# A sum of squares over partitions as two one-pass products of its exact halves

## The chip, the cores and the metric

The kernel runs on one core of one Trainium2 chip. The metric is the device time of one execution in microseconds (us), as the median of several runs. The engines are named TensorE (PE, its weight loads PEld), VectorE (DVE), ScalarE (ACT), GpSimd (POOL) and SyncE (SP).

## The reference

Two consecutive layers of a decoder, on one sequence of 512 tokens of width 1024 in fp32. Layer 0 has four differential-attention heads (A), four forgetting-attention heads (B) and a gate; layer 1 has eight dilated-window heads (C) and a gate. Each layer ends in an output projection, a residual add and a per-layer embedding. The part that matters here is the end of a differential head: two softmax maps are subtracted, applied to the values, and each token's 128 outputs are normalised by the root of their mean square.

```
w = probs(q1b, k1) - lam * probs(q2b, k2)
oa = einsum('bhqk,bkhd->bqhd', w, v)
oa = rms_norm(oa, subln_g) * (1.0 - lam_init)   # mean of squares over 128 values
```

## The kernel before, in words

All large products are made from exact halves. An fp32 operand is split (`split`, L140 to L147) into `hi`, a copy by ScalarE to the type float32r, and `lo`, the remainder, subtracted by VectorE; `mm3` (L173) then adds three float32r products, hi hi, hi lo and lo hi. Each of these is one pass of TensorE over 512 columns. Plain fp32 products remain for transposes, for probabilities times values (L503) and for the normalisation of the differential heads (L521).

The work is a list of jobs (`add_chunk`, L902 to L951). A job is a projection of 512 columns, cut into units, mostly four: one unit is 24 products into one PSUM buffer of the tag U (three buffers, `psU`), and an evacuation, for the query and key units in `qk_post`: L379 copies the PSUM tile to `raw`, L381 squares it. While a job runs, the weights of the next are loaded and split (L143, L144 for layer 0), and heads of attention advance by stages: scores (`scores`, L438, PSUM tag S, two buffers), exponentials (L448), the division by their sums (L480 to L487), transposes (L493, L495), and the product with the values (L503) into PSUM `po`.

`run_jobs` and `slot` fix the order in which the program is written: a slot runs what was deferred to it (`defer`), some attention stages by a planner of costs (`attend`), a share of the weight preparation, then the unit. A scheduler of the framework then orders the instructions of each engine by this order and by its own estimate of when each is ready; each engine executes its queue in order. Work tiles of 128x512 fp32 come from one pool, `t2` (L69), with nine buffers (`T2BUFS`).

When the fourth query block of a differential head is done, `finish_a` (L513) runs. L515 copies `po` to `oc`, L517 squares it to `sq`, both on ScalarE in t2 tiles. One slot later `rest` multiplies `sq` by `onesd`, a 128x128 tile of 1/128 (L118, filled by POOL at L119): the fp32 product L521, in a buffer of the tag S, leaves each token's mean square in all partitions. L523 (VectorE) adds the epsilon, L525 and L526 (ScalarE) take the logarithm and the exponential, giving `y`. One slot later `last` refines `y` by one Newton step (`newton`, L125 to L128) and L531 writes the normalised head. This happens four times, once per A head, between 107 and 189 us of the span, while the projections of the B heads' values, queries and keys run. The heads' results are used by the gate units (L712) much later.

Of the kernel before, what the change touches and what calls it, by code (L numbers as in the profile page):

```python
# [13 lines left out]
F32R = mybir.dt.float32r  # L14
I32 = mybir.dt.int32
AF = mybir.ActivationFunctionType
# [3 lines left out]
P = 128  # L20
# [27 lines left out]
def trunk_kernel(  # L48
# [7 lines left out]
    V, A, G, T = nc.vector, nc.scalar, nc.gpsimd, nc.tensor  # L56
# [8 lines left out]
    def nm(s):  # L65
        cnt[0] += 1
        return f"{s}{cnt[0]}"

    def t2(shape=(P, 512), dt=F32):  # L69
        return sb.tile(list(shape), dt, tag="t2", bufs=T2BUFS, name=nm("t2_"))  # L70
# [10 lines left out]
    def psS():  # L81
        return psum.tile([P, 512], F32, tag="S", bufs=SB, name=nm("ps_"))

    def psX():
        return psum.tile([P, 4, P], F32, tag="X", bufs=XB, name=nm("px_"))

    def psO():
        return psum.tile([P, 512], F32, tag="O", bufs=OB, name=nm("po_"))

    def const(shape, name, dt=F32):  # L90
        return cpool.tile(list(shape), dt, tag=name, name=name)
# [25 lines left out]
    rrow = const([P, 512], "rrow")  # L117
    onesd = const([P, P], "onesd")  # L118
    G.memset(onesd, 1.0 / P)  # L119
    gcols = const([P, 2, KS], "gcols")  # L120
    A.dma_start(out=gcols, in_=norm_g.rearrange("l (k q) -> q l k", q=P))


    def newton(y, ms, tmp):
        V.tensor_tensor(tmp, y, y, op=OP.mult)  # L125
        V.tensor_tensor(tmp, tmp, ms, op=OP.mult)
        V.tensor_scalar(tmp, tmp, -0.5, 1.5, op0=OP.mult, op1=OP.add)
        V.tensor_tensor(y, y, tmp, op=OP.mult)  # L128
# [11 lines left out]
    def split(hi, lo, src, gain=None):  # L140

        if gain is not None:
            A.activation(hi, src, AF.Copy, scale=gain)  # L143
            V.scalar_tensor_tensor(lo, src, gain, hi.bitcast(F32), op0=OP.mult, op1=OP.subtract)  # L144
            return
        A.activation(hi, src, AF.Copy)  # L146
        V.tensor_tensor(lo, src, hi.bitcast(F32), op=OP.subtract)  # L147
# [51 lines left out]
    def defer(n, f):  # L199
        later.setdefault(clock[0] + n, []).append(f)  # L200
# [237 lines left out]
    def scores(qk, qk0, hh, p0, pn, i, bias, pt):  # L438
        n = P * (i + 1)
        ps = psS()  # L440
        if i == 0:
            T.matmul(ps[:, :n], qk0[p0:p0 + pn, 0, hh], qk0[p0:p0 + pn, 1, hh], start=True, stop=True)
        else:
            scores_split(ps, qk, hh, p0, pn, i)
        st_ = sm(3)
        V.tensor_tensor_reduce(out=pt, in0=ps[:, :n], in1=bias, scale=1.0, scalar=BIG,  # L446
                               op0=OP.add, op1=OP.min, accum_out=st_[:, 0:1])
        A.activation(pt, pt, AF.Exp, bias=st_[:, 0:1], scale=-1.0, accum_out=st_[:, 1:2])  # L448
        return st_

    def head_steps(kind, hh, qk, qk0, v, vcol, fin, first, extra=None):
        box = {}

        def ptile():
            return sb.tile([P, 512], F32, tag="P", bufs=PBUFS, name=nm("P"))

        def step(i):
            n = P * (i + 1)
            off = 384 - P * i
            if kind == "b":  # L460
                ck, cq, h = extra
                if i == 0:
                    box["ck"] = t2()
                    nc.sync.dma_start(out=box["ck"], in_=ck[h:h + 1, :].broadcast_to((P, 512)))
                bt = t2()
                V.scalar_tensor_tensor(bt[:, :n], box["ck"][:, :n], cq[:, i, h:h + 1],
                                       consts["causal"][:, off:512], op0=OP.subtract, op1=OP.add)
                bias = bt[:, :n]
            else:
                bias = consts["causal" if kind == "a" else "biasc"][:, off:512]  # L470
            p1 = ptile()[:, :n]
            if kind == "a":
                p2 = ptile()[:, :n]
                s1 = scores(qk, qk0, hh, 0, 64, i, bias, p1)
                s2 = scores(qk, qk0, hh, 64, 64, i, bias, p2)
            else:
                s1 = scores(qk, qk0, hh, 0, P, i, bias, p1)

            def end():
                V.reciprocal(s1[:, 2:3], s1[:, 1:2])  # L480
                if kind == "a":
                    V.reciprocal(s2[:, 2:3], s2[:, 1:2])
                    V.tensor_tensor(s2[:, 2:3], s2[:, 2:3], consts["lam"], op=OP.mult)
                    G.tensor_scalar(p2, p2, s2[:, 2:3], 0.0, op0=OP.mult, op1=OP.add)
                    V.scalar_tensor_tensor(p1, p1, s1[:, 2:3], p2, op0=OP.mult, op1=OP.subtract)
                else:
                    G.tensor_scalar(p1, p1, s1[:, 2:3], 0.0, op0=OP.mult, op1=OP.add)  # L487
                defer(LAG2, stage2)

            def stage2():  # L490
                px = psX()
                for j in range(i + 1):
                    T.transpose(px[:, j, :], p1[:, j * P:(j + 1) * P], ident)  # L493
                pt = sb.tile([P, 4, P], F32, tag="pt", bufs=PTBUFS, name=nm("pt"))
                A.activation(pt[:, :i + 1, :], px[:, :i + 1, :], AF.Copy)  # L495
                defer(LAG3, lambda: stage3(pt))

            def stage3(pt):
                if i == 0:
                    box["o"] = psO()  # L500
                po = box["o"]
                for j in range(i + 1):
                    T.matmul(po[:, i * P:(i + 1) * P], v[:, j, vcol:vcol + P], pt[:, j, :],  # L503
                             start=(j == 0), stop=(j == i))
                if i == 3:
                    if kind == "a":
                        finish_a(po)
                    else:
                        A.activation(fin, po, AF.Copy)

            return end

        def finish_a(po):  # L513
            oc = t2()
            A.activation(oc, po, AF.Copy)  # L515
            sq = t2()
            A.activation(sq, oc, AF.Square)  # L517

            def rest():
                pm = psS()  # L520
                T.matmul(pm, onesd, sq, start=True, stop=True)  # L521
                ms = sq
                V.tensor_single_scalar(ms, pm, EPS, op=OP.add)  # L523
                y = t2()
                A.activation(y, ms, AF.Ln)  # L525
                A.activation(y, y, AF.Exp, scale=-0.5)  # L526

                def last():
                    tmp = t2()
                    newton(y, ms, tmp)  # L530
                    V.scalar_tensor_tensor(fin, oc, consts["subg"], y, op0=OP.mult, op1=OP.mult)  # L531

                defer(1, last)

            defer(1, rest)

        for i in range(4):
            cost = (i + 1) * (0.76 if kind == "a" else 0.55)
            queue.append((first[i], cost, lambda i=i: step(i)))
# [443 lines left out]
```

## Time and profile before

| what | value |
|---|---|
| median of 3 runs | 708.09 us (707.98 to 708.30) |
| the profiled execution | 709.72 us, span 707.9 us |
| TensorE busy | 689.8 us (97%), weight loads 80% |
| VectorE, ScalarE, GpSimd busy | 64%, 57%, 28% |
| granted TensorE clock, mean | 0.995 of full speed |

The span goes from the first to the last instruction; the 1.8 us between it and the execution's time lie outside. Busy shares are averages over the whole span. A busy TensorE is not TensorE at its peak, since products overlap and their ends are modelled.

### The profile page before, as it was taken

To read this page: it belongs to the slowest core of one execution; us is meant where nothing else is said; L and a number is where in the kernel's file an instruction comes from. 1 tells how busy PE (TensorE), PEld (TensorE's weight loads), DVE (VectorE), ACT (ScalarE), POOL (GpSimd) and SP (SyncE) were. 2 spreads that over 40 slices of the span, in tenths; PEclk is the share of its full clock that TensorE was granted. 3 is DMA by queue.
4 is the path that set the end of the run, shared out by engine and by line. 5 is a ranking of instruction groups with operands and counts; after the bars stand their busy time and mean duration, and the time that the engine had idled before them with its cause. 6 is when DMAs were issued, how large, how long until landed. Compare 5 with 4: busy or idle time off the path is not lost.

```text
span 707.9 us, 9982 instructions
## 1 busy us (share of the span) xinstructions
PE 689.8 (97%) x3424; PEld 569.5 (80%) x3424; DVE 451.6 (64%) x1045; ACT 403.2 (57%) x849; POOL 201.7 (28%) x406
## 2 busy tenths in 40 slices
PE   6999999999999999899999999999999999999997
PEld 4887777777788887688888788888888888888886
DVE  3558668747977989664655475824668585654242
ACT  5746665727667882334675555755748686444220
POOL 3884321100002347300341134302344236500000
PEclk9999999999999999899999999999999999999999
DMA  8533140301341321223404311303123031343111
GB/s 261 146 91 119 31 120 1 91 30 52 97 121 31 118 74 51 83 86 95 144 6 149 120 58 62 120 3 118 44 76 120 1 119 31 90 133 122 59 59 46
DMA packets 45876, 59.74 MB, mean 84 GB/s; under 512 B 8061, under 2 KB 25981, under 8 KB 45825
## 3 DMA queue, kind: packets, MB, share of 16 engines
q1 hardware_dynamic: 43760, 59.09, 27.0%
q8 instruction: 27, 0.44, 0.2%
q10 hardware_dynamic: 2064, 0.01, 0.2%
q14 instruction: 25, 0.20, 0.1%
HBM read 56.98 MB, written 2.11 MB: 83 GB/s over the span
## 4 chain that ended last, share of the span: by engine, by line
PE 92%; DVE 3%; DMA 2%; ACT 1%; POOL 1%; issue 1%; SPq 0%; DVEq 0%; ACTq 0%
PE pu L176 12%; PE pu L174 12%; PE pu L175 12%; PE po L503 5%; PE pu_g L176 4%; PE pu_g L174 4%; PE pu_g L175 4%; PE pu_v L174 4%; PE pu_v L175 4%; PE pu_v L176 4%; PE pu_o L174 4%; PE pu_o L175 4%; PE pu_o L176 4%; PE ps L174 3%; PE ps L175 2%; PE ps L176 2%
## 5 line engine op out<-in xcount | busy, mean ns | idle before, releaser
L144 DVE SCALAR_TENSOR_TENSOR wl<-raw,gcols,wh 128x512 fp32r<-128x512 f32 x128 | 95.5, 780 | 23.1 <-ACT wh L143 22.9
L174 PE MATMUL pu<-wh,ar 128*128 128x512 f32 x256 | 101.7, 397 | 0.0
L175 PE MATMUL pu<-wl,ar 128*128 128x512 f32 x256 | 101.1, 395 | 0.0
L176 PE MATMUL pu<-wh,ar 128*128 128x512 f32 x256 | 100.7, 394 | 0.0
L143 ACT ACTIVATE wh<-raw,gcols 128x512 fp32r<-128x512 f32 x128 | 85.0, 722 | 20.1 <-DMA raw<-in_w_in_even_dram 11.7
L487 POOL TENSOR_SCALAR P<-P,sm 128x128 f32<-128x128 f32 (+3 forms) x48 | 30.9, 647 | 132.9 <-DVE sm L480 98.3
L448 ACT ACTIVATE P<-P,sm 128x128 f32<-128x128 f32 (+3 forms) x80 | 44.7, 559 | 33.5 <-DVE sm L446 31.9
L174 PEld LDWEIGHTS pu<-wh,ar 128*128 128x128 f32 x256 | 48.1, 188 | 11.1 <-issue 1.3
L147 DVE TENSOR_TENSOR wl<-raw,wh 128x1024 fp32r<-128x1024 f32 x36 | 47.8, 1339 | 14.2 <-ACT wh L146 13.7
L176 PEld LDWEIGHTS pu<-wh,ar 128*128 128x128 f32 x256 | 48.1, 188 | 10.0
L175 PEld LDWEIGHTS pu<-wl,ar 128*128 128x128 f32 x256 | 48.1, 188 | 9.4 <-issue 0.3
L174 PE MATMUL pu_o<-ar,wh 128*128 128x512 f32 x128 | 50.4, 402 | 4.3 <-ACT ar L146 4.3
L174 PE MATMUL pu<-ar,wh 128*128 128x512 f32 x136 | 53.8, 396 | 0.4 <-ACT t L381 0.4
L176 PE MATMUL pu<-ar,wl 128*128 128x512 f32 x136 | 54.2, 398 | 0.0
L175 PE MATMUL pu<-ar,wh 128*128 128x512 f32 x136 | 53.9, 396 | 0.0
L176 PE MATMUL pu_v<-wh,ar 128*128 128x512 f32 x128 | 52.2, 409 | 0.0
L174 PE MATMUL pu_v<-wh,ar 128*128 128x512 f32 x128 | 51.3, 403 | 0.7 <-DVE t L694 0.7
L175 PE MATMUL pu_v<-wl,ar 128*128 128x512 f32 x128 | 51.5, 402 | 0.0
L175 PE MATMUL pu_o<-ar,wh 128*128 128x512 f32 x128 | 51.2, 400 | 0.0
L176 PE MATMUL pu_o<-ar,wl 128*128 128x512 f32 x128 | 51.0, 398 | 0.0
L146 ACT ACTIVATE wh<-raw 128x1024 fp32r<-128x1024 f32 x36 | 38.0, 1058 | 19.5 <-DMA raw<-in_w_ple_dram 6.4
L146 ACT ACTIVATE ar<-t 128x512 fp32r<-128x512 f32 (+1 forms) x41 | 25.3, 618 | 40.1 <-DVE t L739 18.8
(235 smaller groups left out, 1623.4 us busy)
## 6 DMA issues: line engine op xcount, KB each, us to landing
raw<-in_w_in_even_dram SPq DMA_DIRECT2D x16, 512.0 KB, 5.2
raw<-in_w_in_even_dram SPq DMA_DIRECT2D x32, 256.0 KB, 3.2
raw<-in_w_ple_gate_dram SPq DMA_DIRECT2D x16, 512.0 KB, 4.7
raw<-in_w_in_odd_dram SPq DMA_DIRECT2D x16, 512.0 KB, 4.2
raw<-in_w_in_odd_dram SPq DMA_DIRECT2D x32, 256.0 KB, 3.1
raw<-in_w_out_even_dram SPq DMA_DIRECT2D x8, 512.0 KB, 4.2
raw<-in_w_out_odd_dram SPq DMA_DIRECT2D x8, 512.0 KB, 3.8
ar<-in_x_dram SPq DMA_DIRECT2D x8, 256.0 KB, 6.7
```

What stands on the lines that cost most here:

```text
L143: A.activation(hi, src, AF.Copy, scale=gain)
L144: V.scalar_tensor_tensor(lo, src, gain, hi.bitcast(F32), op0=OP.mult, op1=OP.subtract)
L146: A.activation(hi, src, AF.Copy)
L147: V.tensor_tensor(lo, src, hi.bitcast(F32), op=OP.subtract)
L174: T.matmul(ps, lh, rh, start=first, stop=False)
L175: T.matmul(ps, lh, rl, start=False, stop=False)
L176: T.matmul(ps, ll, rh, start=False, stop=last)
L448: A.activation(pt, pt, AF.Exp, bias=st_[:, 0:1], scale=-1.0, accum_out=st_[:, 1:2])
L487: G.tensor_scalar(p1, p1, s1[:, 2:3], 0.0, op0=OP.mult, op1=OP.add)
L503: T.matmul(po[:, i * P:(i + 1) * P], v[:, j, vcol:vcol + P], pt[:, j, :], start=(j == 0), stop=(j == i))
```

## The change

The sum of squares is made by two one-pass float32r products instead of one fp32 product. A tile `onesr` holds the 1/128 in float32r (1/128 is a power of two, so nothing is lost), copied once at the start by ScalarE. `sq` is split into its two parts right after it is made, with two more t2 tiles; the two products add up in the same PSUM buffer.

```diff
@@ -117,6 +117,8 @@
     rrow = const([P, 512], "rrow")
     onesd = const([P, P], "onesd")
     G.memset(onesd, 1.0 / P)
+    onesr = const([P, P], "onesr", F32R)
+    A.activation(onesr, onesd, AF.Copy)
     gcols = const([P, 2, KS], "gcols")
     A.dma_start(out=gcols, in_=norm_g.rearrange("l (k q) -> q l k", q=P))
@@ -513,12 +515,14 @@
         def finish_a(po):
             oc = t2()
             A.activation(oc, po, AF.Copy)
-            sq = t2()
+            sq, parts = t2(), [t2(dt=F32R) for _ in range(2)]
             A.activation(sq, oc, AF.Square)
+            split(*parts, sq)
 
             def rest():
                 pm = psS()
-                T.matmul(pm, onesd, sq, start=True, stop=True)
+                for i, part in enumerate(parts):
+                    T.matmul(pm, onesr, part, start=i == 0, stop=i == 1)
                 ms = sq
                 V.tensor_single_scalar(ms, pm, EPS, op=OP.add)
                 y = t2()
```

## Rows read from the trace of the kernel before

**Rows 1.** The page: busy time by engine, and the ending chain's shares by engine.
```profile
PE 689.8 (97%) x3424; PEld 569.5 (80%) x3424; DVE 451.6 (64%) x1045; ACT 403.2 (57%) x849; POOL 201.7 (28%) x406
...
PE 92%; DVE 3%; DMA 2%; ACT 1%; POOL 1%; issue 1%; SPq 0%; DVEq 0%; ACTq 0%
```

**Rows 2.** The instructions of L521: count, ns min/median/max, first and last start, forms.
```profile
L521 PEld LDWEIGHTS ps<-t,onesd x8: 186/190/192, 121.6 to 180.5; 128*128 128x128 f32 x8
L521 PE MATMUL ps<-t,onesd x8: 592/594/697, 121.7 to 181.0; 128*128 128x512 f32 x8
```

**Rows 3.** The chain in order of time, 120 to 165 us: start, us, what.
```profile
121.86 0.86 PE ps L521 x2
...
129.71 0.23 PE pu_v L174
...
162.60 0.43 PE ps L174
```

**Rows 4.** What TensorE waited for, whole span: us in total, times, longest.
```profile
PE pu_o L174 <- ACT ar L146: 4.3, 1, 4.3
...
PE pu L174 <- ACT t L381: 0.4, 1, 0.4
...
PE ps L521 <- ACT t L517: 0.2, 1, 0.2
```

**Rows 5.** Groups by line and shape: busy us, mean ns | idle before.
```profile
L147 DVE TENSOR_TENSOR ar<-t,ar 128x512 fp32r<-128x512 f32 x39 | 28.7, 744 | 14.8 <-ACT ar L146 14.7
...
L146 ACT ACTIVATE ar<-t 128x512 fp32r<-128x512 f32 x39 | 24.5, 629 | 37.6 <-DVE t L739 18.8 <-POOL t L712 11.7 <-DVE t L787 7.1
```

**Rows 6.** Timeline of ScalarE at the start: start us, us, instruction, [idle before].
```profile
4.80 0.60 ACT L146 ACTIVATE ar<-px 128x512 fp32r<-128x512 f32 x1 [2.78 <-PE px L210]
```

**Rows 7.** The products of L174 between 135 and 165 us (8 per unit).
```profile
L174 PE MATMUL pu<-wh,ar x24: 387/389/502, 135.6 to 158.3; 128*128 128x512 f32 x24
```

**Rows 8.** Timeline around the third head, 158.9 to 165.1 us.
```profile
158.98 1.05 PE L503 MATMUL po<-pt,ar 128*128 128x128 f32 x8
...
160.07 0.60 ACT L515 ACTIVATE t<-po 128x512 f32<-128x512 f32 x1 [3.36 <-PE po L503]
...
161.50 1.10 PE L521 MATMUL ps<-t,onesd 128*128 128x512 f32 x2
...
163.36 0.63 ACT L525 ACTIVATE t<-t 128x512 f32<-128x512 f32 x1 [0.34 <-DVE t L523]
...
163.90 0.58 ACT L379 ACTIVATE t<-pu 128x512 f32<-128x512 f32 x1
...
164.38 0.59 ACT L381 ACTIVATE t<-pu 128x512 f32<-128x512 f32 x1
...
165.02 0.50 PE L174 MATMUL pu<-wh,ar 128*128 128x512 f32 x1
```

**Rows 9.** Timeline around the fourth head, 177 to 182 us.
```profile
177.94 1.16 PE L503 MATMUL po<-pt,ar 128*128 128x128 f32 x8 [0.21 <-ACT pt L495]
...
179.65 0.63 PE L411 MATMUL px<-ident,t 128*128 128x128 f32 x4 [0.55 <-DVE sm L125]
179.76 0.63 ACT L517 ACTIVATE t<-t 128x512 f32<-128x512 f32 x1
...
180.30 0.58 ACT L379 ACTIVATE t<-pu 128x512 f32<-128x512 f32 x1
...
181.13 0.60 ACT L381 ACTIVATE t<-pu 128x512 f32<-128x512 f32 x1
...
181.40 0.60 PE L411 MATMUL px<-ident,t 128*128 128x128 f32 x4
...
181.78 0.50 PE L174 MATMUL pu<-wh,ar 128*128 128x512 f32 x1
```

**Rows 10.** Timeline of ScalarE after the fourth head.
```profile
187.83 0.60 ACT L379 ACTIVATE t<-pu 128x512 f32<-128x512 f32 x1 [1.91 <-DVE t L128]
```

**Rows 11.** Timeline of the weight loader after the third head's L521.
```profile
162.53 0.18 PEld L174 LDWEIGHTS ps<-ar 64*128 64x128 f32 x1 [0.76 <-DVE sm L480]
```

## The prediction

> **What bounds the kernel now.** I read the page first: TensorE is busy 97% of the span, VectorE 64%, ScalarE 57%, and TensorE carries 92% of the chain that ended last [rows 1]. The reader should see an engine with no room of its own, so that time taken off TensorE counts and time added elsewhere counts only where TensorE then waits. Second, the line of the statistic's product, L521: four products stand in the trace as eight records of 594 ns with eight weight loads [rows 2]; one full fp32 product is two passes of the records, each with its load. Third, the chain in order of time, for what they hold TensorE for: the first head's pair takes 0.86 us, the second head's (at 134.72 us) the same, while a one-pass 128x512 product in a running stream takes 0.23 us, and 0.43 us right after another kind of product [rows 3]. Fourth, the whole list of what TensorE waited for: the one wait over 1 us after the start is 4.3 us at an output projection, a later stage than the change, and at L521 it waited once, 0.2 us [rows 4]. Last, the timelines around the four heads, which the sum needs because there TensorE stands close to a second limit.
>
> **The parts.** Four heads, one finish each.
>
> *The product.* Removed: 0.86 us a head. Added: two one-pass products, at best 2 x 0.23 = 0.46 us, at worst 0.43 + 0.23 = 0.66 us [rows 3]. The gain is 0.20 to 0.40 us a head. I take 0.40, since both products read one stationary tile and stand together, as the running stream does. If nothing else moved, 4 x 0.40 = 1.6 us would go.
>
> *The split.* Per head one ScalarE copy to fp32r (629 ns) and one VectorE subtraction (744 ns) on a 128x512 SBUF tile [rows 5]; over four heads 2.5 us and 3.0 us, on engines 43% and 36% idle. As work they cost nothing: TensorE's backlog covers them, and without it they would cost their 1.37 us per head. As latency they stand between the squares and the second product: the subtraction waits for the copy, with the next block's minimum pass (L446) queued behind it on VectorE, and the second product for the subtraction, with that block's scores queued behind it on TensorE. Both move with the head's chain, and are in its price below.
>
> *The rounded ones.* One 128x128 ScalarE copy at the start, no longer than the 629 ns of the larger one. ScalarE sits idle 2.78 us before its first copy at 4.80 us [rows 6]. It waits for POOL's fill of the ones, one of POOL's first instructions, and the load of the norm gains stands behind it on ScalarE's queue if the order stays as written; the gains are first used behind that first copy. I cost it at 0, and at most at its 0.6 us.
>
> *Two more t2 buffers per head.* The pool has nine. They are taken between the squares (L516) and whatever the program asks for next, and this is where the latency meets TensorE. Three units of the next projection are on TensorE from 135.6 to 158.3 us [rows 7] and fill all three psU buffers; the fourth starts only at 165.02, right as L381 (164.38 + 0.59) ends [rows 8]. ScalarE was idle 3.36 us before 160.07, yet the evacuation L379 runs only at 163.90, behind L525. My reading is that t2 buffers are handed out in program order, so the `raw` of that unit comes after the third head's `y`, which L525 writes. So the third head's chain sets when the projection may go on.
>
> Step by step for heads one and two, where TensorE never waits: -0.40 each, -0.8 us. Head three: from the squares to L525 the chain now holds the 1.10 us of L521 [rows 8]. After the change it holds the copy 0.63, the subtraction 0.74 and the second product at 0.43 (the first runs beside the subtraction): 0.63 + 0.74 + 0.43 - 1.10 = +0.7 us. The fourth unit's start moves by -0.8 + 0.7 = -0.1 us. TensorE would have been ready 0.4 us sooner still; head three's gain is lost in a new wait for L381.
>
> Head four: the products of `po` at 177.94 already wait 0.21 us for ScalarE, which comes from VectorE's split of the next weights. That work started at the scores (0.8 us earlier), and VectorE has one more 0.74 us subtraction ahead of it, so it too arrives about 0.1 us earlier. Then L517, L379 0.54 us later, L381, and the next unit at 181.78, 0.05 us after L381's end [rows 9]. The new copy goes between L517 and L379, so L379 moves by 0 (if it is placed ahead) to 0.54 + 0.74 us (if it is placed behind the subtraction too). I take 0.54, the copy alone, as ScalarE's queue keeps order and VectorE's does not bind it. The unit then starts at -0.1 + 0.54 = +0.44 us. The fourth pair of products falls into that wait and gives nothing.
>
> Behind 182 us TensorE's work is unchanged. **Sum: about +0.4 us.** The profiled execution took 709.72 us, 1.82 around its span of 707.9 and 1.63 above the median of 708.09; the difference carries over, 708.09 + 0.44 = **708.5 us**. Ends: the full gain, 706.5; or the worse product price on two heads (+0.4) and L379 behind the subtraction (+0.74), 709.7.
>
> **Rivals.** *The whole gain passes* (706.5 us). If the planner places L379 and L381 ahead of the new split, or the evacuations hang on something else than t2's order, TensorE gives back nothing. For it: at L521 and at L381 TensorE has waited 0.2 and 0.4 us in the whole run [rows 4]. Against it: the two starts that follow an evacuation by 0.05 us [rows 8, 9]. Chance 0.27.
>
> *Slower: t2 runs out at head four.* That the nine can run out there the trace shows: at 187.83 us ScalarE stood 1.91 us before an L379 until VectorE's L128 let a buffer go [rows 10]. At 180 us I count, after the change, oc, sq, hi and lo of head four, the `raw` whose transposes run at 181.40, the row tile of the first forgetting head and the `raw` and `sq` of the unit to be evacuated [rows 9]: eight of nine. It decides from ten on, if the planner holds two more (the bias tile of that head, or the `raw` whose transposes run at 179.65). Then L379 waits until the products have read hi and lo: from L517's end 180.39 copy 0.63, subtraction 0.74, product 0.43, then L379 0.48 and L381 0.59 (their distances at head three), which is 183.26 in place of 181.78 for the unit: +1.48 - 0.1 = +1.4 us, and some hundredths for each hand-over: 709.6 us. For it: the wait at 187.83. Against it: the count, which leaves one free. Chance 0.20.
>
> *The product gets no shorter* (709.3 us). Both forms make two weight loads per head, so a TensorE paced by loads would gain nothing and heads one and two lose their 0.8: 708.5 + 0.8. The row speaks against it: after L521's two loads at head three the loader stood idle 0.76 us [rows 11], so the passes, not the loads, filled the time. Chance 0.05. The Trainium skill, page "Perfetto Trace Analysis", section "Identifying the Most-Contended Engine", says to judge TensorE by the busy share of its weight loads (with its share of peak arithmetic) rather than of its products; by that rule, at 80% loads [rows 1], a fifth of this engine is free and the 1.6 us would be worth little. The idle row does not bear it out at this line.
>
> **How the numbers follow.** My forecast has 0.48. What a measurement of this kernel can tell from no change is about 0.2%, 1.4 us: below 706.7 is faster, above 709.5 slower. Faster: 0.24 of the first rival and 0.03 of the forecast's own edge, as a new order of instructions can also shorten a wait: 0.27. Slower: 0.16 of the second rival, 0.01 of the third, 0.06 of the forecast where both upper prices meet: 0.23. Same: 0.50. The forecast's own range is 708.0 (L379 ahead of the split at head four) to 709.7; the range that should hold 8 in 10 takes in the full gain and the case of the full pool, each with some tenths for the hand-overs, 706.4 to 710.2.
>
> **What would show it.** Right: two records per head, each well under 594 ns, on the product's line; 0.4 us less on the chain at heads one and two; the units behind heads three and four starting right at the end of an L381, with a TensorE wait for ScalarE of some half a microsecond there. Wrong: L379 ahead of the split, and no new wait (then the first rival); an L379 behind the products at head four, waiting for a buffer (the second); records of 594 ns again (the third). It would also be wrong if differences arise behind 190 us, where nothing of the change runs: then the order of instructions moved, and my sum has no term for that.

## The result, and the profile after

The changed kernel takes 712.58 us (median of 4 runs, 711.87 to 714.00) where the kernel before took 708.04 us beside it (4 runs, 707.83 to 708.30). The ratio is 1.0063, interval [1.0050, 1.0076]: slower by 0.6%, 4.1 us above the forecast of 708.5 and outside the predicted range of 706.4 to 710.2. The profiled execution took 714.00 us, the longest of the four; its span is 712.2 us, its mean granted clock 0.992 (before 709.72, 707.9 and 0.995). In the changed file the lines stand two lower from L121 on (`mm3` is L176 to L178, the evacuations are L381 and L383, the product of `po` is L505), and in the finish the copy of `po` is L517, the squares L519, the split L148 (copy) and L149 (subtraction), the statistic's product L525, the epsilon step L527, logarithm and exponential L529 and L530.

The page's busy times and the chain's shares by engine, which answer to [rows 1]:

```profile
PE 690.7 (97%) x3424; PEld 571.7 (80%) x3424; DVE 454.8 (64%) x1049; ACT 405.6 (57%) x854; POOL 200.2 (28%) x406
...
PE 85%; DVE 6%; ACT 3%; DMA 2%; issue 1%; POOL 1%; SPq 0%; DVEq 0%; POOLq 0%; ACTq 0%
```

By busy shares nothing happened. The chain tells more: TensorE's share fell from 92% to 85%, and VectorE's and ScalarE's rose from 3% and 1% to 6% and 3%. They now set TensorE's pace somewhere.

The product's own line did what was wanted (instructions of L525, then the first head's pair in the chain of waits; [rows 2, 3] before):

```profile
L525 PEld LDWEIGHTS ps<-t,onesr x8: 186/187/192, 121.5 to 185.0; 128*128 128x128 f32 x8
L525 PE MATMUL ps<-t,onesr x8: 395/486/503, 121.5 to 185.0; 128*128 128x512 f32 x8
...
121.79 0.47 PE ps L525 x2
```

At head one the pair holds TensorE 0.47 us instead of 0.86, at head two twice 0.23. Where this was given back, and more, shows when the first product of each stage starts (read from the two timelines):

| start of | before, us | after, us | difference |
|---|---|---|---|
| the third head's products of `po` | 158.98 | 158.13 | -0.85 |
| the unit behind head three | 165.02 | 166.66 | +1.64 |
| the next unit | 170.95 | 175.03 | +4.08 |
| the unit behind head four | 181.78 | 186.35 | +4.57 |
| the output projection | 261.36 | 265.81 | +4.45 |
| the output projection's last 24 products; from there to the end the difference stays | 312.12 | 316.32 | +4.20 |

Heads one and two gain 0.85 us. Head three loses 2.49, the unit behind it 2.44, head four 0.49. Behind it the difference stays between 3.7 and 6.0 us, as units stand in another order, and ends near where it began.

The stages do not hold the same work. The six products of `po` that stood at 175.73 us, in the second of the two units, stand at 173.89 in the first one now, where they take 0.67 us; the first one's three transposes, 0.33 us, moved ahead of it. Like for like the unit behind head three loses 2.1 us, not 2.44, and head four 1.2, not 0.49.

What TensorE waited for, whole span (us in total, times, longest; [rows 4] before). The waits for L148, L448 and L149 at `ps` are new; that for L497 at `po` was 0.2 us, that for L383 at `pu` 0.4:

```profile
PE pu_o L176 <- ACT ar L148: 5.4, 2, 4.2
PE ps L525 <- ACT t L148: 1.1, 1, 1.1
PE po L505 <- ACT pt L497: 1.1, 1, 1.1
PE pu L176 <- ACT t L383: 0.8, 1, 0.8
...
PE ps L176 <- DVE sm L448: 0.4, 1, 0.4
PE ps L525 <- DVE t L149: 0.2, 1, 0.2
```

The timeline of the changed kernel around the third head ([rows 8] before):

```profile
159.85 0.63 ACT L519 ACTIVATE t<-t 128x512 f32<-128x512 f32 x1
...
160.60 0.61 ACT L450 ACTIVATE P<-P,sm 128x384 f32<-128x384 f32 x1
161.21 0.36 ACT L497 ACTIVATE pt<-px 128x256 f32<-128x256 f32 x1
...
161.48 0.62 ACT L148 ACTIVATE t<-t 128x512 fp32r<-128x512 f32 x1
161.63 0.71 PE L505 MATMUL po<-pt,ar 128*128 128x128 f32 x4 [1.13 <-ACT pt L497]
...
162.12 0.69 DVE L149 TENSOR_TENSOR t<-t,t 128x512 fp32r<-128x512 f32 x1 [0.62 <-ACT t L148]
162.15 0.49 PE L525 MATMUL ps<-t,onesr 128*128 128x512 f32 x1
162.57 0.50 PE L176 MATMUL ps<-ar 64*128 64x512 f32 x1
...
163.46 0.50 PE L525 MATMUL ps<-t,onesr 128*128 128x512 f32 x1
...
164.18 0.69 DVE L527 TENSOR_SCALAR t<-ps 128x512 f32<-128x512 f32 x1
...
165.03 0.61 ACT L529 ACTIVATE t<-t 128x512 f32<-128x512 f32 x1
...
165.54 0.58 ACT L381 ACTIVATE t<-pu 128x512 f32<-128x512 f32 x1
...
166.02 0.58 ACT L383 ACTIVATE t<-pu 128x512 f32<-128x512 f32 x1
...
166.66 0.80 PE L176 MATMUL pu<-wh,ar 128*128 128x512 f32 x1
```

The end is as forecast: logarithm, L381, L383, and the unit at once behind it. The length is not. From the start of the squares to the logarithm it was 2.66 us before (160.70 to 163.36); it is 5.18 us (159.85 to 165.03). The added work is a small part of that growth of 2.5 us: copy 0.62, subtraction 0.69 and second product 0.50 stand where the 1.10 us of the old pair stood, +0.71 us. The other 1.8 us are queueing. The copy starts 1.0 us after the squares, behind an exponential and a transpose copy on ScalarE; the second product stands behind a block's three score products (162.57 on) on TensorE, 0.65 us after its operand was ready; the epsilon step stands 0.2 us behind the next minimum pass on VectorE, and the logarithm 0.2 us behind the next exponential.

TensorE itself was hardly earlier. It had waited 1.13 us for the transpose copy L497 and 0.36 us for the minimum pass L448, and three transposes had come ahead of the unit; the weight load of the unit's first product then waited only 0.27 us for L383:

```profile
166.66 0.29 PEld L176 LDWEIGHTS pu<-wh,ar 128*128 128x128 f32 x1 [0.27 <-ACT t L383]
```

So by this trace a shorter finish alone would have let the unit start some 0.3 us earlier at most: two paths are late here, and both run through places in queues.

And one thing more. The windows of all engines over this place (length, busy us and instructions by engine, granted clock, DMA share, GB/s):

```profile
158.00:162.00 4.00, 2.87 (x23) 2.28 (x22) 1.69 (x6) 2.63 (x7) 0.00 (x0) 1.00 0.00 0
162.00:166.00 4.00, 3.64 (x13) 1.92 (x12) 2.83 (x9) 2.39 (x7) 0.59 (x1) 0.80 0.00 0
166.00:170.00 4.00, 4.00 (x11) 3.08 (x12) 3.85 (x11) 3.56 (x9) 0.64 (x1) 0.50 0.00 0
170.00:174.00 4.00, 4.00 (x17) 3.23 (x16) 3.62 (x6) 3.26 (x8) 0.41 (x1) 0.85 0.00 0
```

TensorE was busy 2.87 of 4.00 us, then the granted clock fell to 0.50, the 1.2 GHz level, and stayed there from about 164 to 171 us. Before, it was 1.00 throughout. The first eleven products of the unit behind head three took 2.63 us before and take 4.72 now: that is the 2.1 us.

One difference behind the heads is no clear effect of the change. In both kernels TensorE stands idle for over 4 us at the output projection (4.3 us before, 4.2 now), and the clock falls there too. The windows, first of the kernel before, then of the changed one:

```profile
284.00:288.00 4.00, 2.16 (x5) 1.66 (x6) 1.20 (x1) 0.63 (x1) 2.40 (x2) 0.51 0.14 55
288.00:292.00 4.00, 4.00 (x13) 3.11 (x13) 3.29 (x6) 2.20 (x4) 0.54 (x1) 0.64 0.00 0
```

```profile
288.00:292.00 4.00, 1.04 (x3) 0.84 (x3) 1.06 (x1) 0.63 (x1) 3.52 (x3) 0.83 0.37 126
292.00:296.00 4.00, 4.00 (x15) 3.12 (x14) 2.54 (x5) 1.61 (x3) 0.00 (x0) 0.74 0.00 0
```

By these means the clock stood at 0.50 for 6.8 us before and for 3.4 us now. Executions of the kernel before differ among themselves in this way too (third batch). The changed kernel has another wait of 1.2 us there, so the two about cancel.

### The profile page after: what moved, and what is told of

Same layout as the page of the kernel before. It is cut to its first block, busy times and chain, and to the rows that moved or that the text cites. A ratio compares the mean times of both kernels' runs of the same rounds, so it can differ in the third digit from the quotient of the medians.

```text
span 712.2 us, 9988 instructions
## 1 busy us (share of the span) xinstructions
PE 690.7 (97%) x3424; PEld 571.7 (80%) x3424; DVE 454.8 (64%) x1049; ACT 405.6 (57%) x854; POOL 200.2 (28%) x406
## 4 chain that ended last, share of the span: by engine, by line
PE 85%; DVE 6%; ACT 3%; DMA 2%; issue 1%; POOL 1%; SPq 0%; DVEq 0%; POOLq 0%; ACTq 0%
PE pu L176 11%; PE pu L178 11%; PE pu L177 11%; PE pu_v L176 4%; PE pu_v L178 4%; PE pu_v L177 4%; PE pu_g L176 4%; PE pu_g L178 4%; PE pu_g L177 4%; PE po L505 4%; PE pu_o L176 4%; PE pu_o L177 3%; PE pu_o L178 3%; PE ps L176 3%; PE ps L177 2%; PE ps L178 2%
## 5 line engine op out<-in xcount | busy, mean ns | idle before, releaser
L146 DVE SCALAR_TENSOR_TENSOR wl<-raw,gcols,wh 128x512 fp32r<-128x512 f32 x128 | 95.2, 779 | 23.5 <-ACT wh L145 23.3
L176 PE MATMUL pu<-wh,ar 128*128 128x512 f32 x256 | 102.6, 401 | 0.8 <-ACT t L383 0.8
L178 PE MATMUL pu<-wh,ar 128*128 128x512 f32 x256 | 101.4, 396 | 0.0
L176 PEld LDWEIGHTS pu<-wh,ar 128*128 128x128 f32 x256 | 48.6, 190 | 12.2 <-ACT t L383 1.4
L149 DVE TENSOR_TENSOR wl<-raw,wh 128x1024 fp32r<-128x1024 f32 x36 | 49.2, 1375 | 13.9 <-ACT wh L148 13.3
L178 PEld LDWEIGHTS pu<-wh,ar 128*128 128x128 f32 x256 | 48.6, 190 | 10.0
L176 PE MATMUL pu_o<-ar,wh 128*128 128x512 f32 x128 | 50.0, 400 | 5.4 <-ACT ar L148 5.4
L178 PE MATMUL pu<-ar,wl 128*128 128x512 f32 x136 | 54.1, 398 | 0.0
L176 PE MATMUL pu<-ar,wh 128*128 128x512 f32 x136 | 53.8, 395 | 0.0
L176 PE MATMUL pu_v<-wh,ar 128*128 128x512 f32 x128 | 51.3, 403 | 0.7 <-DVE t L698 0.7
L178 PE MATMUL pu_v<-wh,ar 128*128 128x512 f32 x128 | 51.7, 405 | 0.0
L178 PE MATMUL pu_o<-ar,wl 128*128 128x512 f32 x128 | 50.8, 397 | 0.0
L148 ACT ACTIVATE wh<-raw 128x1024 fp32r<-128x1024 f32 x36 | 38.1, 1058 | 20.6 <-DMA raw<-in_w_ple_gate_dram 6.7
L148 ACT ACTIVATE ar<-t 128x512 fp32r<-128x512 f32 (+1 forms) x41 | 25.2, 618 | 40.4 <-DVE t L743 18.1
```

The costliest lines, as they stand in the source:

```text
L176: T.matmul(ps, lh, rh, start=first, stop=False)
L178: T.matmul(ps, ll, rh, start=False, stop=last)
```

## The experiments

The kernel before ran beside each batch: 708.91, 708.68, 708.40 and 708.05 us in the four. The starts are those of the two units that stood behind heads three and four (before 165.02 and 181.78). In all_claimed and all_claimed_before both of them start ahead of the head's own product, in rest_2_slots, pm_in_x and delay_only the second one does, so there the start does not tell what the head cost. The column "97 us" is how much later or earlier than in the kernel before TensorE is at the unit that starts at 97.18 us there, ahead of the first head. It arises in the first 19 us, it is there in kernels with no new instruction in front of it (tiles_only), and so it is a difference between executions: take it off the two starts. For the changed kernel it is -0.06 us. Idle and clock are TensorE's over 150 to 210 us (before: idle 1.5 us, mean granted clock 1.00; the changed kernel: 3.7 us and 0.94).

| run | median, us | ratio, interval | 97 us | behind three | behind four | idle | clock |
|---|---|---|---|---|---|---|---|
| rest_2_slots | 711.48 | 1.0037 [1.0023, 1.0051] | -0.81 | 163.55 | 180.01 | 2.5 | 0.97 |
| hi_only | 714.29 | 1.0067 [1.0048, 1.0086] | +0.13 | 167.29 | 185.02 | 3.3 | 0.97 |
| split_unused | 713.64 | 1.0062 [1.0047, 1.0077] | -0.46 | 169.09 | 185.54 | 3.2 | 1.00 |
| pm_in_x | 718.54 | 1.0126 [1.0100, 1.0152] | -0.66 | 166.58 | 178.50 | 6.1 | 0.97 |
| all_claimed | 719.57 | 1.0153 [1.0136, 1.0170] | +0.14 | 159.39 | 182.34 | 5.1 | 0.97 |
| all_claimed_before | 716.69 | 1.0114 [1.0096, 1.0132] | -1.41 | 162.36 | 179.06 | 2.9 | 1.00 |
| delay_only | 718.60 | 1.0129 [1.0101, 1.0156] | -0.70 | 168.25 | 184.08 | 5.4 | 0.97 |
| tiles_only | 708.88 | 1.0003 [0.9993, 1.0013] | -0.81 | 164.71 | 181.20 | 1.4 | 1.00 |
| old_order | 712.12 | 1.0064 [1.0045, 1.0082] | -1.30 | 165.93 | 184.30 | 3.4 | 0.94 |
| new_order_old_work | 713.85 | 1.0082 [1.0068, 1.0096] | -0.21 | 167.85 | 186.38 | 4.3 | 0.97 |
| first_two_heads | 708.35 | 0.9996 [0.9986, 1.0006] | -0.66 | 163.56 | 179.96 | 1.3 | 1.00 |
| rounded_squares | 707.57 | 0.9991 [0.9981, 1.0001] | -0.47 | 162.26 | 179.61 | 2.6 | 1.00 |

**First batch: what in the split costs.** Three theories: L, the latency of the statistic, since its product waits for the split and the evacuation stands behind it; W, the added ScalarE and VectorE work itself; B, the S buffer of PSUM that the pair of products holds while the block's scores wait.

```diff
# rest_2_slots
-            defer(1, rest)
+            defer(2, rest)
# hi_only
-            sq, parts = t2(), [t2(dt=F32R) for _ in range(2)]
+            sq, parts = t2(), [t2(dt=F32R)]
-            split(*parts, sq)
+            A.activation(parts[0], sq, AF.Copy)
-                    T.matmul(pm, onesr, part, start=i == 0, stop=i == 1)
+                    T.matmul(pm, onesr, part, start=True, stop=True)
# split_unused
-                for i, part in enumerate(parts):
-                    T.matmul(pm, onesr, part, start=i == 0, stop=i == 1)
+                T.matmul(pm, onesd, sq, start=True, stop=True)
# pm_in_x
-                pm = psS()
+                pm = psX().rearrange("p a b -> p (a b)")
```

> The products of a head are deferred by two slots in place of one; nothing else differs from the changed kernel. Theory L (latency: behind heads three and four TensorE runs dry because the product waits for copy and subtraction, with all three psU buffers full, and the clock falls for some us): the wait is covered by another slot's work, so 706.3 to 708.0 us and no stretch at half clock near 165 us. Rival W (the extra copy, subtraction and tiles crowd the queues wherever the product stands): 711 to 713. Rival B (the PSUM buffer of the tag S, held from the first product to L527, delays the scores): the buffer is held as long, so 710 to 712.

> Leaves out the low half: no subtraction, one product of the copy, one tile less per head. Theory L: the chain holds one copy (0.63 us) more and a product of 0.5 in place of 1.10, so it is as long as before and TensorE gains 0.63 us a head where it is the bound: 705.5 to 707.5. Rival W: half of the extra work is left, 709.5 to 711. Rival B: the buffer is held from one product to L527, as in the kernel before: 705.5 to 707.5, so this run does not tell L from B.

> Copy, subtraction and the two tiles are made, but nobody reads them: the product is the fp32 one of before, on the squares. Theory L: the product does not wait for the split, so 707.5 to 709. Rival W: all the crowding without the shorter product, 712.5 to 715. Rival B: 707.5 to 709.

> The products write a PSUM buffer of the transposes' tag X in place of the scores' tag S; else the changed kernel. Theory L: the product is as late, the evacuation behind it as well: 710.5 to 713. Rival W: 711 to 713. Rival B: the scores no longer wait, 707 to 709.5.

None of the three holds. B gets no support: out of the S buffers the product is slower still, but there it has a new wait of 2.5 us at L525, behind VectorE's L146, so that the scores' share is not measured. L in its pure form gets none from split_unused, where nothing waits for the split and the time is as long. W met two of its four ranges and missed the others upward; B met one, by rest_2_slots, and L none. What the four have in common is TensorE running dry, each at another place. Here are TensorE's largest waits between 150 and 220 us, first of rest_2_slots, then of split_unused, then of pm_in_x:

```profile
PE pu L176 <- ACT t L383: 1.5, 1, 1.5
PE px L413 <- DVE t L408: 0.9, 1, 0.9
```

```profile
PE po L505 <- ACT pt L497: 1.2, 1, 1.2
PE pu L176 <- ACT t L383: 1.0, 1, 1.0
```

```profile
PE pu L176 <- ACT t L383: 2.7, 1, 2.7
PE px L525 <- DVE ar L146: 2.5, 1, 2.5
```

Deferring the statistic by two slots keeps 0.7 us at head three (163.55, with the 0.81 taken off). The unit at 180.01 then starts after a wait of 1.47 us, at a granted clock of 0.70 over 180 to 185 us, and has the fourth head's product (187.60) inside it, so that the next unit starts at 188.51 (before 187.97): the loss moves. Why four small edits behave so differently shows in the order of TensorE's 3,424 records, set side by side with those of the kernel before by line and tile: the changed kernel differs from it in 49 stretches, rest_2_slots in 63, hi_only in 56, split_unused in 53, pm_in_x in 58. The edit is not put into the old queues; new queues are written.

**Second batch: buffers, work, or the place of the evacuation.** Theory T is the prediction's reading of t2: buffers are handed out in program order, so an evacuation stands behind the finish's requests.

```diff
# all_claimed (all_claimed_before: oc, sq and y alone, in the kernel before)
-            oc = t2()
+            oc, sq, y, parts = t2(), t2(), t2(), [t2(dt=F32R) for _ in range(2)]
+            for s in (oc, sq, y, *parts):
+                G.memset(s[:, 0:1].bitcast(F32), 0.0)
             A.activation(oc, po, AF.Copy)
-            sq, parts = t2(), [t2(dt=F32R) for _ in range(2)]
...
-                y = t2()
# delay_only (kernel before)
             A.activation(sq, oc, AF.Square)
+            A.activation(sq, sq, AF.Copy)
+            V.tensor_single_scalar(sq, sq, 0.0, op=OP.add)
# tiles_only (kernel before)
+            parts = [t2() for _ in range(2)]
+            for s in parts:
+                G.memset(s[:, 0:1], 0.0)
...
+                for s in parts:
+                    G.tensor_scalar(s[:, 0:1], ms[:, 0:1], 1.0, 0.0, op0=OP.mult, op1=OP.add)
```

> The changed kernel, computing the same, but all five t2 tiles of a head's finish (oc, sq, the two parts, y) are requested and touched by one-column POOL fills ahead of the copy of po. Theory T: t2 tiles are handed out in program order, so the evacuation of a projection unit (its tile raw) stands in ScalarE's queue behind the last tile of the head's finish that the program asks for before it; the split made that chain longer, and TensorE, its three psU buffers full, waited at heads three and four. By T the evacuations now go ahead of the chain, the next unit after head three starts by 163 us (166.7 in the changed kernel), no TensorE wait over 0.5 us for L381 or L383 is left between 155 and 190 us, and the time is 705.5 to 708.5 us. Theory W: the added ScalarE and VectorE work itself costs the time on the in-order queues, wherever the evacuations stand: 711 to 713.5 us. Theory D: two more tiles crowd the pool of nine: tiles are now held even longer, 712 us or more.

> The kernel before with its three finish tiles (oc, sq, y) requested early in the same way. Theory T: evacuations ahead of the chain here too; TensorE waits only about 1 us around heads three and four in the kernel before, so 706.8 to 708.3 us, and about 1.6 us (the shorter products) above all_claimed. Theories W and D: no more work and hardly more tiles, 707.5 to 708.5 us.

> The kernel before (fp32 product) with the split's two instructions as work alone: a ScalarE copy of sq in place and a VectorE addition of 0 in place, no tile and no new product. Theory T: head three's chain gets 1.3 to 2.5 us longer ahead of the evacuation that stands behind y, the next unit starts at 166.3 to 167.5 us (165.0 before); at head four the evacuation asks for its tile right after sq, so it is not held by the added work: 709.3 to 711 us. Theory W: as much work as the change, and no shorter product: 712.5 to 715 us. Theory D: no tile more, 708 to 709 us.

> The kernel before with two more t2 tiles per head, filled in one column by POOL and released after the epsilon step; no split, fp32 product. Theory T: the requests are served at once and delay no evacuation: 707.5 to 708.7 us. Theory W: no work of any length, 707.5 to 708.5 us. Theory D: the pool is as crowded as in the change: 711 to 713.5 us.

D falls as a cause of the change's loss: two more tiles alone cost nothing that the medians show (1.0003), where D wants 711 us or more. (By executions of like clock, below, they cost 0.7 us.) T's reading of the buffers fits, and its conclusion does not hold. With the finish's tiles requested early, the evacuation that stood at 165.54 us in the changed kernel runs at 145.90, and the unit behind head three starts at 159.39 (timeline of all_claimed, ScalarE and TensorE):

```profile
145.90 0.60 ACT L381 ACTIVATE t<-pu 128x512 f32<-128x512 f32 x1 [1.54 <-DVE t L128]
...
159.39 0.39 PE L176 MATMUL pu<-wh,ar 128*128 128x512 f32 x1
...
174.82 0.67 PE L176 MATMUL pu<-wh,ar 128*128 128x512 f32 x1 [1.74 <-ACT t L383]
```

But 15 us later TensorE waits 1.74 us for the next evacuation, and 4.7 us in four such waits by 220. My reading is that projections run early are missing later as cover for attention; no run tests it. The kernel before with the same edit loses 8 us although it got no work but three fills of one column; its TensorE idles only 1.4 us more over 150 to 210 us, so that loss is not fully placed. And delay_only, as much work as the split with no new product, is 6 us slower than the change, with a TensorE wait of 2.3 us at an L381. T and W missed their ranges in all three; D's "712 us or more" was met by all_claimed, where five tiles are held for longer, so a crowded pool is not excluded for that run. None of the four says what the work costs, since three got other queues (55, 63 and 53 stretches; tiles_only 19). So the next batch holds the queues.

**Third batch: order and work taken apart.** In two kernels edges that order only the issue hold each engine's queue.

```diff
# old_order: the changed kernel in the queue order of the kernel before, from the second
# head's product on; new_order_old_work: the kernel before in the order of the changed one
     run_jobs()
+    order = {...}
+    traced = list(nc.cur_bb.bb.instructions)
...
+        for p_, n_ in zip(line, line[1:]):
+            tc.add_manual_dep(traced[n_], traced[p_].name, mybir.DependencyInfo(
+                mybir.DependencyClass.NoSync, mybir.DependencyReason.DATA), reason="order")
# first_two_heads
+            first2 = 'heads' not in st or st['heads'] < 2
+            st['heads'] = st.get('heads', 0) + 1
+            sq, parts = t2(), [t2(dt=F32R) for _ in range(2)] if first2 else ()
...
+            if first2: split(*parts, sq)
...
+                if not first2: T.matmul(pm, onesd, sq, start=True, stop=True)
```

> The changed kernel with each engine's queue held, by edges that order issue alone, in the order of the kernel before from the second head's product on; of heads three and four the two products stand at the place of the fp32 product, the copy right behind the square, the subtraction right ahead of the epsilon step (head four: one place earlier). Nothing is left out. Theory O: the framework's scheduler, given the added work, writes each engine's queue in another order, and that order costs the time, not the added work: with the old order 706.5 to 709.5 us, the later units starting within 1 us of the kernel before (165.0, 181.8 us), and no clock below full in 160 to 190 us. Theory W: the added ScalarE and VectorE work and its latency cost the time in any order: 711 to 714 us.

> The kernel before, its work untouched (fp32 product, no split), with each engine's queue held in the order of the changed kernel; the fp32 product stands where the first of the two products stood. Theory O: the order alone costs what the change lost: 710.5 to 714 us, with the loss between 150 and 205 us. Theory W: nothing is added, so 707.3 to 709 us.

> The split and the one-pass products for heads one and two alone, the fp32 product for heads three and four, computing the same; queues as the scheduler writes them, which from head three's product on is the order of the kernel before. Theory O: 0.8 us of TensorE work less and the old order at heads three and four: 706.8 to 708.0 us, below the kernel before. Theory W: half of the added work, half of the loss: 709.5 to 711 us. Nothing passes (the gain is lost in a wait behind head three): 707.8 to 708.7 us.

Each theory met its bad case and missed its good one: the new work in the old order costs (1.0064), and the old work in the new order costs (1.0082). In old_order TensorE's wait is at the product itself (largest waits between 160 and 200 us; the first pieces, 0.69 and 0.88 us, are head three's):

```profile
PE ps L525 <- ACT t L148: 2.3, 2, 1.6
PE ps L525 <- DVE t L149: 1.1, 2, 0.9
```

These are 3.4 us of waiting at heads three and four, where the kernel before waited 0.2 us at its product. The granted clock falls behind it as in the changed kernel: 0.74 in 160 to 164 us, 0.50 in 164 to 168. In new_order_old_work no split exists, yet TensorE waits where the order was made for one (160 to 200 us):

```profile
PE pu L174 <- ACT t L381: 1.7, 2, 1.1
PE po L503 <- ACT pt L495: 1.1, 1, 1.1
PE ps L174 <- DVE sm L446: 0.8, 1, 0.8
PE ps L521 <- ACT t L517: 0.5, 1, 0.5
```

The second line is the 1.13 us that the changed kernel shows at 161.63: the products of `po` now stand ahead of the statistic's product on TensorE, and their transpose copy behind an exponential on ScalarE. So the scheduler's answer to the longer chain is about as dear as the wait that it avoids.

The two traces also part the growth of head three's chain, from squares to logarithm. First old_order, then new_order_old_work:

```profile
158.61 0.63 ACT L519 ACTIVATE t<-t 128x512 f32<-128x512 f32 x1
...
160.54 0.16 DVE L482 RECIPROCAL sm<-sm 128x1 f32<-128x1 f32 x1 [0.79 <-ACT P L450]
160.62 0.67 DVE L149 TENSOR_TENSOR t<-t,t 128x512 fp32r<-128x512 f32 x1
...
162.60 0.63 ACT L529 ACTIVATE t<-t 128x512 f32<-128x512 f32 x1 [1.23 <-DVE t L527]
```

```profile
160.48 0.63 ACT L517 ACTIVATE t<-t 128x512 f32<-128x512 f32 x1
...
165.37 0.69 DVE L523 TENSOR_SCALAR t<-ps 128x512 f32<-128x512 f32 x1
...
166.21 0.61 ACT L525 ACTIVATE t<-t 128x512 f32<-128x512 f32 x1
```

It is 2.66 us in the kernel before, 3.99 with the split in the old order, 5.18 in the changed kernel, and 5.73 in the new order with no split at all. In the old order the split adds 1.33 us, and 0.72 of them are again a place in a queue: the copy ends at 159.90, and the subtraction stands behind a reciprocal that waits for an exponential. In the new order the old product ends at 163.83 and its epsilon step comes 1.54 us later, behind a minimum pass. An order made for one kernel is no neutral ground for the other, so the two prices are not parts of one sum. Nor was the kernel before run with its own order held, so what the edges cost by themselves is not measured.

first_two_heads agrees with it from the other side. With the split at heads one and two alone, little of TensorE's queue moves (15 stretches, in tiles_only 19), none of it behind 156 us, and the gain passes heads three and four: 163.56 and 179.96 are 1.5 and 1.8 us early, 0.8 and 1.2 us with the 0.66 us taken off, and 0.75 us are left at 312 us: the product time of two heads. The median shows no difference, 708.35 against 708.40; that is the range of "nothing passes", and above O's. Sorted by mean granted clock, 9 of the 17 executions of the kernel before have 0.997 (their mean is 708.0 us) and 8 have 0.994 or 0.995 (709.3); of the 11 of first_two_heads one has 0.997, one 0.996, and the other nine have a mean of 708.5. At the lower clock it is 0.8 us ahead; it is at the lower clock more often, which so few executions cannot tell from chance. Sorted in the same way, tiles_only is 0.7 us behind (nine executions at 0.997 with a mean of 708.8, six of the kernel before beside it with 708.0). That is a reading of the runs, not an experiment.

The traces show what the two clocks are: the stretch at 0.50 at the output projection. It lasts 6.8 us in the profiled executions of the kernel before and of first_two_heads (both 0.995), and 3.4 us in that of tiles_only (0.997), behind a wait of 4.3 to 4.6 us each time. Why it is one or the other is open.

**Last: the short product with no split.**

```diff
# rounded_squares
-            sq, parts = t2(), [t2(dt=F32R) for _ in range(2)]
+            sq = t2(dt=F32R)
             A.activation(sq, oc, AF.Square)
-            split(*parts, sq)
...
-                for i, part in enumerate(parts):
-                    T.matmul(pm, onesr, part, start=i == 0, stop=i == 1)
-                ms = sq
+                T.matmul(pm, onesr, sq, start=True, stop=True)
+                ms = t2()
```

> One float32r product per head on the squares as ScalarE writes them in float32r: no split, no low half. The low half of the squares, cut off by the rounding, is left out of the mean; the epsilon step writes to a t2 tile of its own. The queues as the scheduler writes them; they differ from those of the kernel before in few places and agree again behind head four. Theory T (what costs is the split's latency in front of the statistic at heads three and four, and the new order of the queues that it brings): the product gets 4 x 0.63 = 2.5 us shorter and nothing is put in front of it, so 705.3 to 707.3 us, no TensorE wait of over 0.5 us between 150 and 190 us, and the unit after head three starts 1.5 to 2.5 us earlier than in the kernel before (165.0). Rival E (a shorter product gains nothing, since TensorE's time saved is eaten by the wait of some 4 us ahead of the output projection and the lower clock behind it): 707.8 to 709 us.

707.57 us against 708.05, 0.9991 [0.9981, 1.0001]: just above T's range, and just below E's. T's two signs came nearly: one wait of 0.65 us, for VectorE at 178.19, is over its 0.5, and the unit behind head three starts 2.8 us early, 2.3 with the 0.47 us taken off, where three products got 3 x 0.63 = 1.9 us shorter. So without the split's latency the gain passes head three whole. From head four on it is 2.2 us (179.61), or 1.7, after waits for evacuations of 1.1 us in three pieces. At the output projection TensorE waits as long as ever, 4.3 us, so the lead stays. The profiled execution, 704.9 us of span, is 3.0 us shorter than that of the kernel before, and 0.8 of them come from the clock at the output projection, at 0.50 for 3.4 us in place of 6.8. The median keeps 0.5 us. Four of its 11 executions have a clock of 0.996, the profiled one with its short stretch among them; 8 of the 15 beside it have 0.997. Group against group it is ahead by 1.1 us (706.7 against 707.8) and by 0.8 us (707.9 against 708.8), and its share of short ones cannot be told from chance. This version has the lowest median of all, and by less than its interval can prove. An exact version that beats the kernel before was not found.

## Why the prediction was wrong

*The product*, -0.40 us a head: right at heads one and two, 0.47 and 0.46 us for the pair where I took 0.46 (0.86 before). At heads three and four the two products do not stand together, and each starts alone behind other work (records of 0.49 and 0.50 us). Rival three is out, with records of 486 ns in the median. The Trainium skill, page "Perfetto Trace Analysis", section "Identifying the Most-Contended Engine", would judge TensorE's room by the share of its loads, beside its share of peak arithmetic. Here the number of loads and their 80% stayed and the pair got 0.39 us shorter, so at this line the trace does not bear it out.

*Heads one and two*, -0.8: right, -0.85.

*The rounded ones*, 0: right; the copy ran at 2.03 us, and ScalarE stood idle 2.51 us behind it.

*t2 in program order*: the reading fits. all_claimed moved the evacuation from 165.54 to 145.90 by early requests (and the scheduler's new queues). The second rival's full pool did not come: at head four L381 ran at 185.20 us, with the second product (185.00) still at work on its part, and waited for no buffer.

*Head three*, +0.7: this is the step that failed. The four terms of its sum were right: 0.62 + 0.69 + 0.50 - 1.10 = +0.71 us. The chain also got to L381 through the logarithm as I wrote. But I added the durations as if each engine stood free when its operand came. Measured is +2.5 us from the squares to the logarithm (2.66 to 5.18), and the missing 1.8 us are places in three in-order queues. The prediction names them as "queued behind it", says that "both move with the head's chain", and puts them at nothing. In the old order the chain grows by 1.33 us, 0.72 of it in one such place. TensorE's own queue, with the wait of 1.13 us for L497, has no term in the sum either, and it was late by nearly as much.

*A term that is missing*: what a wait costs behind itself. The unit behind head three ran at 0.50 of full clock for most of its length, 2.1 us. I had priced waits by their length alone.

*Head four*, +0.54 on top: 0.49 us in the table, by luck. I had L381 move by one copy. On ScalarE the copy and three instructions of other heads went ahead of it:

```profile
182.94 0.63 ACT L519 ACTIVATE t<-t 128x512 f32<-128x512 f32 x1
183.60 0.63 ACT L148 ACTIVATE t<-t 128x512 fp32r<-128x512 f32 x1
...
185.20 0.60 ACT L381 ACTIVATE t<-pu 128x512 f32<-128x512 f32 x1
```

It starts 2.26 us behind the squares, before 0.54 us. From the head's first product of `po` to the next unit it is 5.35 us, before 3.84, with waits for L148 and L149 at L525 (1.14 and 0.22 us) and for L383 (0.84). The 1.5 us became 0.5 because the stage in front got 1.0 us shorter; 0.67 of that are the six products that had moved into the unit before.

*The order of the queues* was taken as it was; the prediction names a new order only as something that would break it, with differences behind 190 us as the sign. They came (3.7 to 6.0 us), the order did move, and new_order_old_work prices it alone at +0.8%. Whether the changed kernel's 4.5 us are to be put down to the work or to the order has no answer in parts: either alone gives about the whole, and each was run in a queue made for the other. What the runs show is that the split is the cause at heads three and four, with the queues that it brings: without it (rounded_squares) or with it at heads one and two alone nothing is lost.

The sum that the trace supports is -0.85 + 2.49 + 2.44 + 0.49 - 0.37 = +4.20 us; the last term holds the shorter stretch of low clock at the output projection, which is chance as far as the runs tell. The first rival (the whole gain passes) failed by the same step; the second named the right side, for a wrong reason.

Left open: why all_claimed_before loses more than TensorE's idle time shows, what sets the length of the low clock at the output projection, and whether the 2.1 us at head three come in every execution: two of the four have a mean clock of 0.994 and took 711.9 us, and are not traced. A pool of its own for the finish's tiles was not tried.

## What to carry to other kernels

Before a shorter instruction is bought with a longer chain, look for the places where the bottleneck engine has no backlog, and price the chain there with the queue of every engine that it crosses: here 0.7 us of work were 2.5 us of latency. Where a scheduler orders the queues, a small edit may rewrite all of them; hold the old order once, and run the old work in the new order once, before any instruction is blamed. And do the edit where it is hidden: at heads one and two it gained what was computed, at three and four it lost six times that. When two single executions are set side by side, look first at where they stand ahead of the first changed instruction: here they differed by up to 1.4 us there, as much as the gain that was sought.

## What the hardware showed that I had not expected

Waits of 1.13 and 0.36 us at head three, with TensorE busy 2.87 of 4.00 us, were followed by some 7 us at 0.50 of full clock (1.2 GHz): 2.1 us lost on one unit, more than the waits. In rest_2_slots it was 0.70 over 180 to 185 us behind a wait of 1.47 us, in old_order 0.50 over 164 to 168; in split_unused, after 1.24 us at 168.40, it did not fall. And executions of one kernel differ by it: the kernel before has either 0.997 or about 0.995 as its mean clock, 1.3 us apart in the mean, nearly the 1.6 us that all four shorter products together could save. Behind the same wait of some 4.5 us at the output projection the clock stood at 0.50 for 3.4 us in one traced execution and for 6.8 us in another.
